# From norm 2 to the FFN: factors per token tile on VectorE, weight sums and splits made earlier, and a fixed order

## The chip, the core and the metric

The kernel runs on one core of one Trainium2 chip. A time is device microseconds (us) of one execution. The engines are TensorE (PE in the profile, its weight loads PEld), VectorE (DVE), ScalarE (ACT), GpSimd (POOL) and SyncE (SP, which here issues DMA loads).

## The reference

One layer (DEPTH = 1) over 1024 tokens of 1024 channels, float32. The part that matters here is the end of the mixer and the FFN:

```python
merged = (jax.nn.sigmoid(ga) * (y_a @ w_branch_a[l])
          + jax.nn.sigmoid(gb) * (y_b @ w_branch_b[l]))
x = x + g1 * (merged @ w_out[l])                       # output projection
h = rmsnorm(x, ln2_g[l]) * (1.0 + sc2) + sh2           # norm 2
f = (jax.nn.silu(h @ w_ffn_gate[l]) * (h @ w_ffn_up[l])) @ w_ffn_down[l]
x = x + g2 * f
```

Ahead of it stand a first norm, one input projection, stick-breaking attention (`y_a`, 16 heads) and a short gated convolution (`y_b`). The FFN's hidden width is 2816.

## The kernel before

*Split products.* Every float32 operand of a matmul is kept as two fp32r tiles: `hi`, a copy rounded by ScalarE, and `lo`, the difference, made by VectorE. A 128-deep slice of a product is three matmuls: hi x hi, hi x lo, lo x hi. `split` does this for a 512-wide piece of a weight (ScalarE L952, VectorE L953), `split_big` for activations in pieces of 1024 elements (ScalarE L963, VectorE through the helper `tt`, L128).

*The branch projection.* The second attention output is read back from DRAM in 16 tiles (`yr`, L901, two buffers, SyncE's queue), split, and multiplied by `w_a` in eight steps `m`. In one of these steps `preload_wo` loads the first pieces of the output projection's weight and splits them ahead, so that their loads stand on SyncE's queue in between.

*Output projection and norm 2.* The loop runs over two column halves `ch` and eight token tiles `i` of 128 tokens; a tile is 24 matmuls. In the second half, VectorE makes the scaled product `tm` (L1011) and the residual `x1` (L1018) of each tile. ScalarE stores the latter, squares it with a running sum (L1022) and scales it (L1024) by a root that GpSimd makes (`rstd_of`, L114 and L115). `norm2_tail` follows one tile later: eight transposes on TensorE (L971), and eight evictions into `h2b`, taken in turn by ScalarE (L979) and VectorE (L976).

*The FFN's products.* Gate and up are done by a scheme of the Strassen type. `h2b[e][n]` is the quadrant of channel half `e` and token half `n`. Seven factors `rh[q]`/`rl[q]` are made of the four quadrants; factors 0 and 1 are the first token half as it is. The others need differences: for tokens of the second half GpSimd makes two per token tile (the result `t2f` is a tile of its own), another 2048-wide one (L1089) and VectorE the last (L1092), and then `split_big` makes the factors in the order 5, 4, 2, 6, 3. `wsum` makes the four sums `s1` to `s4` of a column's weight tiles: VectorE for the first gate column, GpSimd for all others. A half product (`half_prod`, L123 to L125) is 12 matmuls, and a column of gate or up (`strassen`) is seven of them. Of three columns the two products that need only factors 0 and 1 are made ahead of the rest (`pre`), interleaved with the last token tiles' norm.

*The column loop.* `j` runs over 11 pairs of hidden tiles; ScalarE applies Silu to the gate, VectorE multiplies by up, and seven combinations (`fa`, `fb` and others) are stored to DRAM by `put_f` for the down projection.

*Order.* The framework's scheduler chooses the order on each engine from its own model of the durations; instructions with unmet needs then wait on semaphores. `in_order(i0)` instead fixes, for the instructions from number `i0` on, the order on each engine as the program has it. The kernel before calls it once, in an early stage (L310).

Of the kernel before, what the change touches and what calls it, by code (L numbers as in the profile page):

```python
# [16 lines left out]
P = 128  # L17
# [12 lines left out]
def block_kernel(tc, x, x_t, cols, ada_1, ada_2, ada_row, w_q, w_kv, w_v1, w_cg, w_a, w_b, w_o, w_g, w_u, w_d, out):  # L30
# [850 lines left out]
    def preload_wo():  # L881

        for j in range(2):
            raw = wx.tile([P, 1024], F32, tag="raw", bufs=1, name=nm("raw"))
            cn = 1024 - 512 * j
            nc.sync.dma_start(raw[:, :cn], w_o[0, j, :, :cn])
            for k in range(2 - j):
                hi = wx.tile([P, 512], F32R, tag="whi", bufs=3, name=nm("whi"))
                lo = wx.tile([P, 512], F32R, tag="wlo", bufs=3, name=nm("wlo"))
# [19 lines left out]
    for m in range(KT):  # L909
        if m == KT - 1:  # L910
            preload_wo()
# [24 lines left out]
    wp = sw.enter_context(tc.tile_pool(name="wpd", bufs=1, reuse_waits="tile"))  # L936
    s6 = ExitStack()
# [28 lines left out]
    def norm2_tail(i, xn):  # L966
        n, t0 = i // 4, (i % 4) * P
        for g in range(2):
            tr = bank()
            for j in range(4):  # L970
                nc.tensor.transpose(tr[:, j * P:(j + 1) * P], xn[:, (4 * g + j) * P:(4 * g + j + 1) * P], ident)  # L971
            for j in range(4):
                k = 4 * g + j
                o, s = h2b[g][n][:, j, t0:t0 + P], tr[:, j * P:(j + 1) * P]
# [5 lines left out]
        if n:  # L980
            b = lambda e, m: h2b[e][m][:, :, t0:t0 + P]
            nc.gpsimd.tensor_tensor(out=b(0, 1), in0=b(0, 1), in1=b(0, 0), op=ALU.subtract)
            nc.gpsimd.tensor_tensor(out=t2f[:, :, t0:t0 + P], in0=b(1, 1), in1=b(0, 1), op=ALU.subtract)

    tails = []
    for ch in range(2):
        w = [] if ch else list(w_pre)
        for j in range(len(w) // 2, 4):
            raw = load_raw(w_o[ch, j])
            w += [split(raw[:, c * 512:(c + 1) * 512]) for c in range(len(w) % 2, 2)]  # L990
        if ch == 1:
            swx.close()
            rqs.close()
            s5 = ExitStack()
            hp = s5.enter_context(tc.tile_pool(name="phh", bufs=1, side="right", reuse_waits="tile"))

            h2t = {q: hp.tile([P, 4, 512], F32, name=f"h2b{q}") for q in ("01", "11", "t2", "00", "10")}
            h2b = [[h2t[f"{e}{n}"] for n in range(2)] for e in range(2)]
            t2f = h2t["t2"]
        cs = slice(ch * 512, ch * 512 + 512)  # L1000
        for i in range(8):
            n, t0 = i // 4, (i % 4) * P
            xi = dp.tile([P, 512], F32, tag="xr", bufs=3, name=nm("xr"))
            nc.scalar.dma_start(xi, x[i * P:(i + 1) * P, cs])
            ps = bank()
            for k in range(KT):
                nc.tensor.matmul(ps, mh[n][:, k, t0:t0 + P], w[k][0], start=(k == 0), stop=False)
                nc.tensor.matmul(ps, mh[n][:, k, t0:t0 + P], w[k][1], start=False, stop=False)
                nc.tensor.matmul(ps, mlo[n][:, k, t0:t0 + P], w[k][0], start=False, stop=(k == KT - 1))
            tm = dp.tile([P, 512], F32, tag="tm", bufs=2, name=nm("tm"))  # L1010
# [12 lines left out]
            r = rstd_of(ss, 1.0 / D, dp, 1)  # L1023
            nc.scalar.activation(xn, x1, AF.Copy, scale=r[:, 0:1])  # L1024
# [10 lines left out]
    rh = [bh[:, 0:4], bh[:, 4:8], None, None, None, None, None]  # L1035
    rl = [bl[:, 0:4], bl[:, 4:8], None, None, None, None, None]
    NJ = NH // 2

# [4 lines left out]
    pre = {}  # L1043
    for key, src in (((0, 0), w_g), ((0, 1), w_u), ((1, 0), w_g)):
        raw = load_raw(src[key[0]])
        ps = bank()
        prod(ps, split(raw[:, :512]), 0)
        p2 = bank()
        prod(p2, split(raw[:, 512:]), 1)
        if tails:  # L1050
            norm2_tail(*tails.pop())
        pre[key] = (ps, p2)

    def wsum(j, e, src, eng):

        raw = load_raw(src[j])
        a11, a12 = raw[:, :512], raw[:, 512:]
        if (j, e) in pre:
            p1, p2 = pre[j, e]
        else:  # L1060
            p1, p2 = bank(), bank()
            prod(p1, split(a11), 0)
# [289 lines left out]
```

## Time and profile before

| | |
|---|---|
| median of 3 runs | 1936.05 us (1933.06 to 1937.56) |
| the profiled execution | 1933.53 us, its span 1931.8 us |
| TensorE busy | 1838.2 us, 95% |
| its weight loads | 1517.6 us, 79% |
| VectorE busy | 1452.0 us, 75% |
| ScalarE busy | 865.7 us, 45% |
| GpSimd busy | 484.4 us, 25% |
| mean granted clock of TensorE | 0.983 |
| DMA | 235 MB read, 111 MB written, 180 GB/s |

How to read the rows. A row of a timeline has the start in us from the span's start, the length of the instruction or the mean of a run of equal ones, the engine, line, operation, result and operands by name, shape, and the count; in brackets stands the wait ahead of it and what ended it. L123 to L125 are the matmuls of the FFN's half products, L1009 those of the output projection, L772 and L773 those of the branch projection; the line of VectorE's helper, L128, stands for many places, so that names and shapes tell them apart. A row of windows gives for a stretch its length, then busy time and instructions of TensorE, its weight loads, VectorE, ScalarE and GpSimd, then the mean granted clock, the share of the DMA engines, and the count of something that isn't used here.

### The profile page before, as it was taken

The numbers are of one execution on the slowest core, as the hardware profiler recorded it, in microseconds if no ns is written. First come the engines' busy times: TensorE is split into PE (matmuls) and PEld (weight loads), VectorE is DVE, ScalarE is ACT, GpSimd is POOL, SyncE is SP. The second block draws the span as 40 slices with busy tenths as digits, with TensorE's granted clock in tenths as the row PEclk, the third lists the DMA queues.
The fourth block names the chain that finished last, engine by engine and source line by source line (L and its number), as shares of the span: only waits on it lengthen the run. The fifth ranks groups of instructions, "written<-read, shape, count | busy, mean of one in ns | idle before, by whom it ended". The sixth has DMA issues, their size and how long they took to land.

```text
span 1931.8 us, 25024 instructions
## 1 busy us (share of the span) xinstructions
PE 1838.2 (95%) x8829; PEld 1517.6 (79%) x8829; DVE 1452.0 (75%) x2024; ACT 865.7 (45%) x1602; POOL 484.4 (25%) x349
## 2 busy tenths in 40 slices
PE   7799898999999899999999899979999999999999
PEld 5578776888778888887888688867888888878787
DVE  7864676878784799999999644499988788843854
ACT  4332443333333677777777321464444434422221
POOL 0484335532321000000000000055445445301013
PEclk9899998999999899999999999999999999999999
DMA  7655432224676666569653535323444334389666
GB/s 293 221 179 185 169 132 97 88 77 164 228 242 219 187 168 180 170 177 296 188 159 108 186 136 193 138 85 116 157 161 167 153 139 165 132 308 332 253 222 224
DMA packets 151148, 347.47 MB, mean 180 GB/s; under 512 B 15088, under 2 KB 52208, under 8 KB 149104
## 3 DMA queue, kind: packets, MB, share of 16 engines
q1 hardware_dynamic: 74000, 218.80, 34.4%
q10 hardware_dynamic: 76016, 123.41, 17.8%
q0 software_dynamic: 1008, 3.67, 0.5%
q8 instruction: 70, 1.15, 0.2%
q14 instruction: 54, 0.44, 0.1%
HBM read 235.19 MB, written 110.62 MB: 179 GB/s over the span
## 4 chain that ended last, share of the span: by engine, by line
PE 62%; DVE 16%; DMA 9%; issue 5%; POOL 4%; ACT 3%; ACTq 0%; SPq 0%; DVEq 0%; POOLq 0%
PE e L124 6%; PE e L123 6%; PE e L125 6%; PE pj L123 4%; PE pj L124 4%; PE pj L125 4%; PE e L1190 3%; PE e L1191 3%; DVE pt L697 3%; PE e L1189 3%; PE pj L772 3%; PE pj L773 3%; PE pj L774 3%; POOL tb L128 2%; PE pj L269 2%
## 5 line engine op out<-in xcount | busy, mean ns | idle before, releaser
L697 DVE TENSOR_TENSOR_SCAN pt<-pt,dm 128x256 f32<-128x256 f32 (+7 forms) x128 | 171.6, 1344 | 9.6 <-ACT pt L692 9.3
L114 POOL TENSOR_SCALAR rs_m<-ss 128x1 f32<-128x1 f32 x8 | 2.0, 254 | 656.4 <-ACT xn L1022 656.4
L124 PE MATMUL e<-big,whi 128*128 128x512 f32 x352 | 138.1, 392 | 7.6 <-DVE big L128 7.6
L123 PE MATMUL e<-big,whi 128*128 128x512 f32 x352 | 137.6, 391 | 1.0 <-ACT c L1105 1.0
L125 PE MATMUL e<-big,wlo 128*128 128x512 f32 x352 | 137.5, 391 | 0.0
L692 ACT ACTIVATE pt<-z,rq 128x512 f32<-128x512 f32 (+2 forms) x192 | 112.4, 586 | 44.0 <-PE z L691 19.8
L123 PE MATMUL pj<-big,whi 128*128 128x512 f32 x320 | 127.1, 397 | 1.0 <-DVE c L128 1.0
L128 POOL TENSOR_TENSOR ws<-raw,raw 128x512 f32<-128x512 f32 x41 | 58.9, 1437 | 275.6 <-DMA raw<-w_cg 135.2
L125 PE MATMUL pj<-big,wlo 128*128 128x512 f32 x320 | 126.8, 396 | 0.0
L269 PE MATMUL pj<-whi,big 128*128 128x512 f32 x352 | 111.9, 404 | 15.4 <-DVE vs L376 9.8
L1190 PE MATMUL e<-wlo,f 128*128 128x512 f32 (+1 forms) x319 | 123.0, 386 | 3.8 <-DVE wlo L953 3.8
L124 PE MATMUL pj<-big,whi 128*128 128x512 f32 x320 | 126.5, 395 | 0.0
L1191 PE MATMUL e<-whi,f 128*128 128x512 f32 (+1 forms) x319 | 122.4, 384 | 0.0
L128 DVE TENSOR_TENSOR c<-e,c 128x512 f32<-128x512 f32 x154 | 103.0, 682 | 22.6 <-PE e L125 22.5
L1189 PE MATMUL e<-whi,f 128*128 128x512 f32 (+1 forms) x319 | 116.7, 384 | 1.8 <-DMA f<-d_f 1.8
L128 DVE TENSOR_TENSOR c<-pj,c 128x512 f32<-128x512 f32 x140 | 93.5, 684 | 28.6 <-PE pj L125 28.3
L693 ACT ACTIVATE sg<-z,rq 128x512 f32<-128x512 f32 (+1 forms) x192 | 112.3, 588 | 1.1 <-PE tr L713 1.0
L419 ACT ACTIVATE whi<-raw 128x512 fp32r<-128x512 f32 x116 | 72.9, 632 | 86.3 <-PE pj L124 50.9
L128 POOL TENSOR_TENSOR ws<-raw,ws 128x512 f32<-128x512 f32 x62 | 102.5, 1653 | 22.4 <-DVE wlo L953 20.7
L128 DVE TENSOR_TENSOR wlo<-raw,whi 128x512 fp32r<-128x512 f32 x116 | 90.0, 779 | 21.3 <-ACT whi L419 19.8
L713 PE MATMUL tr<-dm,sg 128*128 128x128 f32 x576 | 92.7, 276 | 13.2 <-DVE atl L717 11.0
L124 PE MATMUL e<-rl,whi 128*128 128x512 f32 x264 | 102.8, 389 | 1.8 <-DVE rl L128 1.8
(246 smaller groups left out, 5340.1 us busy)
## 6 DMA issues: line engine op xcount, KB each, us to landing
f<-d_f SPq DMA_DIRECT2D x77, 512.0 KB, 4.4
d_f<-fs ACTq DMA_DIRECT2D x70, 512.0 KB, 2.7
raw<-w_cg SPq DMA_DIRECT2D x40, 512.0 KB, 3.5
uu<-ada ACTq DMA_DIRECT2D x32, 512.0 KB, 4.5
raw<-w_g SPq DMA_DIRECT2D x24, 512.0 KB, 3.1
raw<-w_u SPq DMA_DIRECT2D x23, 512.0 KB, 3.1
d_k<-khl ACTq DMA_DIRECT2D x32, 256.0 KB, 3.3
d_q<-gt ACTq DMA_DIRECT2D x32, 256.0 KB, 2.0
```

The lines of the kernel that those rows point to most:

```text
L123: nc.tensor.matmul(ps, wh[:, k, :], fh[:, k, :], start=(k == 0), stop=False)
L124: nc.tensor.matmul(ps, wh[:, k, :], fl[:, k, :], start=False, stop=False)
L125: nc.tensor.matmul(ps, wl[:, k, :], fh[:, k, :], start=False, stop=(k == 3))
L128: eng.tensor_tensor(out=out, in0=a, in1=b, op=op)
L269: nc.tensor.matmul(ps, a, b, start=(k == 0 and q == 0), stop=(k == KT - 1 and q == 2))
L692: nc.scalar.activation(pt[:, off + s0:off + s0 + m], z[:, :m], AF.Sigmoid, scale=rq[:, 1, i, h:h + 1])
L693: nc.scalar.activation(sg[:, s0:s0 + m], z[:, :m], AF.Sigmoid, scale=rq[:, 0, i, h:h + 1])
L697: nc.vector.tensor_tensor_scan(out=pt[:, rev], data0=pt[:, rev], data1=dm[:, rev], initial=0.0, op0=ALU.mult, op1=ALU.add)
L713: nc.tensor.transpose(tr[:, j * P:(j + 1) * P], sg[:, (b0 + j) * P:(b0 + j + 1) * P], ident)
L1189: nc.tensor.matmul(o, sh, w[0][:, c], start=(j == 0), stop=False)
L1190: nc.tensor.matmul(o, sh, w[1][:, c], start=False, stop=False)
L1191: nc.tensor.matmul(o, sl, w[0][:, c], start=False, stop=(j == NJ - 1))
```

## The change

1. *Branch projection.* `preload_wo` runs one step `m` earlier, and loads three pieces with five splits, instead of two with three.
2. *Weight sums.* The four sums of the first gate column are made by VectorE in the first half of the output projection, into tiles `wt` of a new pool that last to the end of the FFN. The second load of that column's weight comes later for its plain products, so 1 MB of weights is read twice.
3. *Factors.* `tail_f` makes them for each token tile of the second half: five VectorE operations of 128x4x128 and one ScalarE copy. Factor 2 is split there at once, into a pool of its own; the differences are left in `h2b`. GpSimd's differences and `t2f` go.
4. *The last two token tiles.* Tile 6's transposes come inside tile 7's 24 matmuls (at `k == 5`), and its evictions and `tail_f(6)` ahead of VectorE's first operation for tile 7. The split of the second half of the first gate weight stands behind the square of tile 7.
5. *Behind the projection.* The two plain products of three columns, `two(...)`, are made as before; the splits of the four ready sums (`sps`) come in between, and the first gate column's remaining products run in the order 6, 5, 3, 7, 4, each behind its factor.
6. *Fixed order.* `in_order(i0)` covers all this, from the last token tile's start to the split of factor 3.
7. *The column loop.* `c11` of a gate is added up at once and put into `wt` tile 0; `fa` and `fb` go into `wt` tiles 2 and 3.

```diff
-        for j in range(2):
+        for j in range(3):
             raw = wx.tile([P, 1024], F32, tag="raw", bufs=1, name=nm("raw"))
...
-                hi = wx.tile([P, 512], F32R, tag="whi", bufs=3, name=nm("whi"))
+                hi = wx.tile([P, 512], F32R, tag="whi", bufs=5, name=nm("whi"))
...
-        if m == KT - 1:
+        if m == KT - 2:
             preload_wo()
...
+    def tail_f(i, qs=(0, 1)):
+        t0 = (i % 4) * P
+        b = lambda e, m: h2b[e][m][:, :, t0:t0 + P]
+        if 0 in qs:
+            h_, l_ = (r[:, :, t0:t0 + P] for r in (rh[2], rl[2]))
+            tt(nc.vector, b(0, 1), b(0, 1), b(0, 0), ALU.subtract)
+            nc.scalar.activation(h_, b(1, 1), AF.Copy)
+            tt(nc.vector, l_, b(1, 1), h_.bitcast(F32), ALU.subtract)
+            tt(nc.vector, b(1, 1), b(1, 1), b(0, 1), ALU.subtract)
+        if 1 in qs:
+            tt(nc.vector, b(0, 0), b(1, 1), b(0, 0), ALU.subtract)
+            tt(nc.vector, b(1, 0), b(1, 0), b(1, 1), ALU.subtract)
...
-        if n:
-            b = lambda e, m: h2b[e][m][:, :, t0:t0 + P]
-            nc.gpsimd.tensor_tensor(out=b(0, 1), in0=b(0, 1), in1=b(0, 0), op=ALU.subtract)
-            nc.gpsimd.tensor_tensor(out=t2f[:, :, t0:t0 + P], in0=b(1, 1), in1=b(0, 1), op=ALU.subtract)
+        if i > 3:
+            late_f.append(i)
+            while i > 4 and late_f:
+                tail_f(late_f.pop(0))
...
+        if ch == 0:
+            ws0 = [wt(q) for q in range(4)]
+            w_sums(load_raw(w_g[0]), load_raw(w_g[NJ]), *ws0, nc.vector)
...
+            last = (ch, i) == (1, 7)
+            if last:
+                i0 = len(nc.cur_bb.bb.instructions)
+                raw00 = load_raw(w_g[0])
+                s00 = split(raw00[:, :512])
...
             for k in range(KT):
+                if last and k == 5:
+                    trs = tail_tr(tails.pop()[1])
...
+            if last:
+                tail_ev(6, trs)
+                tail_f(6)
             tm = dp.tile([P, 512], F32, tag="tm", bufs=2, name=nm("tm"))
...
             r = rstd_of(ss, 1.0 / D, dp, 1)
+            if last:
+                s00b = split(raw00[:, 512:])
...
+    pq[1], pq[2] = two(s00, s00b)
+    s01 = halves(load_raw(w_u[0]))
+    trs = tail_tr(tails.pop()[1])
...
-    split_big(rh[5], rl[5], t2f)
-    split_big(rh[4], rl[4], h2b[0][1])
-    nc.gpsimd.tensor_tensor(out=h2b[0][0], in0=t2f, in1=h2b[0][0], op=ALU.subtract)
-    split_big(rh[2], rl[2], h2b[1][1])
+    sps = [split(ws0[q]) for q in (1, 0, 3, 2)]
+    pre[0, 1] = two(*s01)
+    x1p, x11 = wt(1), wt(0)
+    nc.scalar.activation(x1p, pq[1], AF.Copy)
+    tt(nc.vector, x11, pq[2], x1p, ALU.add)
+    s10 = halves(load_raw(w_g[1]))
+    tail_ev(7, trs)
+    tail_f(7, (0,))
+    pre[1, 0] = two(*s10)
+    split_big(rh[5], rl[5], h2b[1][1])
+    pq[6] = product(sps[0], 5)
+    split_big(rh[4], rl[4], h2b[0][1])
+    pq[5] = product(sps[1], 4)
+    tail_f(7, (1,))
+    pq[3] = product(sps[2], 2)
     split_big(rh[6], rl[6], h2b[0][0])
-    nc.vector.tensor_tensor(out=h2b[1][0], in0=h2b[1][0], in1=t2f, op=ALU.subtract)
+    pq[7] = product(sps[3], 6)
+    sp4 = split(load_raw(w_g[NJ])[:, 512:])
     split_big(rh[3], rl[3], h2b[1][0])
+    in_order(i0)
...
-        nc.scalar.activation(c11, p1, AF.Copy)
...
-        tt(nc.vector, c11, p2, c11, ALU.add)
+        c11 = ct("c01", 1) if e else wt(0)
...
+        nc.scalar.activation(c21, p1, AF.Copy)
+        tt(nc.vector, c11, p2, c21, ALU.add)
```

The new lines `tail_tr` and `tail_ev` are the two parts of the old `norm2_tail`, and `product` and `two` wrap `half_prod` with a PSUM bank each. Three places show how the instructions move. In these rows a name is followed by its numbers, `e` is a PSUM bank, `raw` a loaded weight, `whi` and `wlo` its split, `rh` and `rl` a factor, `big` a pair of factors.

VectorE at the last token tile, before (`tm_2439` and `x1_2440` are tile 7's):

```order
L1011 TENSOR_TENSOR tm_2439_11962<-e_2438_11937,g1b_11198 128x512
L953 TENSOR_TENSOR wlo_2469_12109<-raw_2463_12088,whi_2468_12108 128x512
L1018 TENSOR_TENSOR x1_2440_11964<-tm_2439_11962,xr_2437_11935 128x512
L976 TENSOR_SCALAR h2b01_11521<-e_2445_11976,a2_11200,mod_104 128x128
L976 TENSOR_SCALAR h2b11_11522<-e_2446_11985,a2_11200,mod_104 128x128
L128 TENSOR_TENSOR raw_2470_12124<-raw_2470_12124,raw_2471_12126 128x512
L128 TENSOR_TENSOR s2_12128<-raw_2471_12126,raw_2470_12124 128x512
L128 TENSOR_TENSOR raw_2471_12126<-raw_2471_12126 128x512
L128 TENSOR_TENSOR raw_2470_12124<-raw_2470_12124,s2_12128 128x512
L976 TENSOR_SCALAR h2b01_11521<-e_2445_11976,a2_11200,mod_104 128x128
L976 TENSOR_SCALAR h2b11_11522<-e_2446_11985,a2_11200,mod_104 128x128
```

VectorE there, after (`tm_2450` and `x1_2451` are tile 7's):

```order
L982 TENSOR_SCALAR h2b01_11541<-e_2448_11986,a2_11213,mod_104 128x128
L128 TENSOR_TENSOR h2b00_11543<-h2b11_11542,h2b00_11543 128x4x128
L128 TENSOR_TENSOR h2b10_11544<-h2b10_11544,h2b11_11542 128x4x128
L982 TENSOR_SCALAR h2b11_11542<-e_2449_11987,a2_11213,mod_104 128x128 x2
L128 TENSOR_TENSOR h2b01_11541<-h2b01_11541,h2b00_11543 128x4x128
L128 TENSOR_TENSOR rl2_11537<-h2b11_11542,rh2_11536 128x4x128
L128 TENSOR_TENSOR h2b11_11542<-h2b11_11542,h2b01_11541 128x4x128
L128 TENSOR_TENSOR h2b00_11543<-h2b11_11542,h2b00_11543 128x4x128
L128 TENSOR_TENSOR h2b10_11544<-h2b10_11544,h2b11_11542 128x4x128
L1064 TENSOR_TENSOR tm_2450_12019<-e_2447_11970,g1b_11211 128x512
L1071 TENSOR_TENSOR x1_2451_12021<-tm_2450_12019,xr_2446_11968 128x512
L955 TENSOR_TENSOR wlo_2457_12033<-raw_2443_11962,whi_2456_12032 128x512
```

Tile 7's two operations stood ahead of tile 6's four evictions (L976) and the four weight sums; now they stand behind tile 6's evictions (L982) and the factor operations of tiles 5 and 6 (128x4x128).

ScalarE from the last residual's store on, before:

```order
L1019 DMA d_x1_80<-x1_2440_11964 128x512
L1022 ACTIVATE xn_2442_11969,ss_2441_11968<-x1_2440_11964 128x1024
L979 ACTIVATE h2b01_11521<-e_2445_11976,mod_104,a2_11200 128x128
L979 ACTIVATE h2b11_11522<-e_2446_11985,mod_104,a2_11200 128x128
L952 ACTIVATE whi_2479_12254<-s2_12128 128x512
L1024 ACTIVATE xn_2442_11969<-x1_2440_11964,rs_r_2444_11972 128x1024
L952 ACTIVATE whi_2482_12273<-raw_2471_12126 128x512
L952 ACTIVATE whi_2485_12291<-raw_2470_12124 128x512
L952 ACTIVATE whi_2488_12310<-raw_2470_12124 128x512
L952 ACTIVATE whi_2491_12328<-raw_2471_12126 128x512
```

And after:

```order
L1072 DMA d_x1_80<-x1_2451_12021 128x512
L1075 ACTIVATE xn_2453_12026,ss_2452_12025<-x1_2451_12021 128x1024
L954 ACTIVATE whi_2456_12032<-raw_2443_11962 128x512
L1079 ACTIVATE xn_2453_12026<-x1_2451_12021,rs_r_2455_12029 128x1024
L954 ACTIVATE whi_2461_12065<-raw_2460_12063 128x512
L954 ACTIVATE whi_2463_12069<-raw_2460_12063 128x512
L954 ACTIVATE whi_2469_12093<-wt_2324_11232 128x512
L954 ACTIVATE whi_2471_12097<-wt_2323_11231 128x512
L954 ACTIVATE whi_2473_12101<-wt_2326_11234 128x512
L954 ACTIVATE whi_2475_12105<-wt_2325_11233 128x512
L1125 ACTIVATE wt_2479_12135<-e_2458_12037 128x512
L1203 ACT_TABLE_LOAD
```

The evictions of tile 6 (L979) stood behind the square; now only a weight split (L954) stands between the square and the scaling of tile 7, and six more splits, a copy and the table load follow ahead of tile 7's evictions.

SyncE in the branch projection, before:

```order
L886 DMA raw_2296_11103<-w_o 128x512
L901 DMA yr_2192_10512<-d_ya0_72 128x512
L901 DMA yr_2194_10517<-d_ya1_73 128x512
L735 DMA d_ya1_73<-oy_2170_10395 64x256
L901 DMA yr_2196_10522<-d_ya1_73 128x512
L901 DMA yr_2198_10527<-d_ya1_73 128x512
L735 DMA d_ya1_73<-oy_2173_10423 64x256
L915 DMA sgi_2215_10567<-d_sga_74 128x512
L901 DMA yr_2200_10532<-d_ya1_73 128x512
```

And after:

```order
L886 DMA raw_2285_11027<-w_o 128x1024
L901 DMA yr_2192_10512<-d_ya0_72 128x512
L901 DMA yr_2194_10517<-d_ya1_73 128x512
L735 DMA d_ya1_73<-oy_2170_10395 64x256
L886 DMA raw_2290_11037<-w_o 128x512
L901 DMA yr_2196_10522<-d_ya1_73 128x512
L735 DMA d_ya1_73<-oy_2173_10423 64x256
L901 DMA yr_2198_10527<-d_ya1_73 128x512
L915 DMA sgi_2215_10567<-d_sga_74 128x512
```

The output weight's pieces (`w_o`) are now three, and the third stands ahead of the third `yr` load behind the second piece.

More of the change, by code (lines that the diff above doesn't have):

```diff
@@ L936, in block_kernel @@
     wp = sw.enter_context(tc.tile_pool(name="wpd", bufs=1, reuse_waits="tile"))
+    stp = ExitStack()
+    tp = stp.enter_context(tc.tile_pool(name="pht", bufs=1, reuse_waits="tile"))
     s6 = ExitStack()
@@ L1096, in block_kernel, with wsum @@
     cp = s7.enter_context(tc.tile_pool(name="phc2", bufs=1, side="right", reuse_waits="tile"))
+    def wsum(j, e, src, eng):
+        raw = load_raw(src[j])
+        p1, p2 = pre[j, e] if (j, e) in pre else two(*halves(raw))
+        raw2 = load_raw(src[j + NJ])
+        ws = [cp.tile([P, 512], F32, tag=f"ws{q}", bufs=1, name=nm("ws")) for q in range(4)]
+        w_sums(raw, raw2, *ws, eng)
+        return (p1, p2, *ws, raw2[:, 512:])
     def ct(tag, bufs):
```

106 lines of the change are left out of this document (57 added, 49 removed).

## The prediction

> **What bounds the kernel now.** I read the page's slices first (TensorE at nine tenths or more except near slice 28), then the 4 us windows of that dip, and then each engine's timeline through it. TensorE from the last tokens of the output projection to the second FFN column:
>
> ```profile
> 1271.40 0.39 PE L1009 MATMUL e<-whi,big 128*128 128x512 f32 x1
> 1272.70 1.09 PE L971 MATMUL e<-dm,xn 128*128 128x128 f32 x8 [0.91 <-ACT xn L1024]
> ...
> 1281.10 1.09 PE L971 MATMUL e<-dm,xn 128*128 128x128 f32 x8 [1.82 <-ACT xn L1024]
> ...
> 1300.58 0.79 PE L124 MATMUL e<-big,whi 128*128 128x512 f32 x1 [7.04 <-DVE big L128]
> 1301.18 0.63 PE L125 MATMUL e<-big,wlo 128*128 128x512 f32 x1
> ...
> 1310.68 0.50 PE L124 MATMUL e<-rl,whi 128*128 128x512 f32 x1 [1.75 <-DVE rl L128]
> ...
> 1318.75 0.39 PE L123 MATMUL e<-big,whi 128*128 128x512 f32 x1
> ...
> 1332.35 0.39 PE L123 MATMUL e<-big,whi 128*128 128x512 f32 x1
> ```
>
> The last two rows are 60 matmuls apart: 0.227 us each. From 1271.6 (end of the projection's issue) to 1318.75 TensorE does 132 matmuls (6 half products ahead, 5 products) and two groups of transposes at 0.85 us: 31.6 us of work in 47.1. So 15.5 us is all that this stage can give back, 0.8% of the time; it is waits for VectorE, and a clock that falls behind the long one:
>
> ```profile
> 1296.00:1300.00 4.00, 0.00 (x0) 0.00 (x0) 4.00 (x2) 1.65 (x2) 4.00 (x3) 0.69 0.00 0
> 1300.00:1304.00 4.00, 3.42 (x8) 2.74 (x9) 4.00 (x3) 2.85 (x4) 3.92 (x3) 0.50 0.00 0
> ```
>
> In both windows VectorE (third busy figure) is at 4.00 of 4.00 and GpSimd (fifth) nearly so; the granted clock is 0.50 in the second. What fills VectorE:
>
> ```profile
> 1256.76 2.36 DVE L128 TENSOR_TENSOR big<-h2b,big 128x1024 fp32r<-128x1024 f32 x2 [0.54 <-ACT big L963]
> ...
> 1265.38 0.69 DVE L1011 TENSOR_TENSOR tm<-e,g1b 128x512 f32<-128x512 f32 x1 [1.11 <-PE e L1009]
> ...
> 1275.88 0.68 DVE L1018 TENSOR_TENSOR x<-tm,xr 128x512 f32<-128x512 f32 x1
> ...
> 1278.77 0.69 DVE L128 TENSOR_TENSOR raw<-raw 128x512 f32<-128x512 f32 x1
> ...
> 1291.69 6.63 DVE L1092 TENSOR_TENSOR h2b<-h2b,h2bt 128x2048 f32<-128x2048 f32 x1
> 1298.24 4.51 DVE L128 TENSOR_TENSOR big<-h2b,big 128x1024 fp32r<-128x1024 f32 x2
> ...
> 1307.14 4.62 DVE L128 TENSOR_TENSOR rl<-h2b,rh 128x1024 fp32r<-128x1024 f32 x4
> ```
>
> ```profile
> 1290.76 5.41 POOL L1089 TENSOR_TENSOR h2b<-h2bt,h2b 128x2048 f32<-128x2048 f32 x1
> 1296.12 3.32 POOL L128 TENSOR_TENSOR ws<-raw,raw 128x512 f32<-128x512 f32 x1
> ```
>
> A 1024-wide split takes 1.15 us with GpSimd idle (1256.76, 1307.14) and 2.25 beside it (1298.24). A 512-wide operation alone starts its follower 0.60 later.
>
> The profiled execution took 1933.53 us (span 1931.8); the runs' median is 1936.05, 2.5 above it. I add the change to both.
>
> **The change, step by step.** What leaves GpSimd (eight 512-wide differences and a 2048-wide one, 12 units of 512) becomes 12 x 0.60 = 7.2 us of VectorE. The weight sums (four times 0.60) move ahead of the stage, to where VectorE waits for TensorE; they cost nothing there while that slack lasts, else 2.4 us. In return VectorE runs beside an idle GpSimd: 6.63 for 2048 elements instead of some 2.4, and 2.2 more for the pair at 1298. The engine's load thus falls a little; what counts is the order, and I walk it with the rows above and these of ScalarE:
>
> ```profile
> 1241.24 1.06 ACT L1022 ACTIVATE xn<-x 128x1024 f32<-128x1024 f32 x1 [0.49 <-DVE h2b L976]
> ...
> 1242.30 0.79 ACT L979 ACTIVATE h2b<-e,mod,a 128x128 f32<-128x128 f32 x2
> 1243.34 1.15 ACT L1024 ACTIVATE xn<-x,rs_r 128x1024 f32<-128x1024 f32 x1 [0.24 <-POOL rs_r L115]
> ...
> 1280.95 2.18 ACT L952 ACTIVATE whi<-raw 128x512 fp32r<-128x512 f32 x4
> ...
> 1298.35 3.90 ACT L963 ACTIVATE rh<-h2b 128x1024 fp32r<-128x1024 f32 x4 [5.62 <-DVE h2b L1092]
> ...
> 1307.93 1.28 ACT L1136 ACT_TABLE_LOAD   x1
> ```
>
> *Token tile 6.* VectorE takes it at 1265.4 as before, but with one factor operation of tile 4 in between: residual done at 1267.2. Then 0.4 for a store's issue, the square 1.2, GpSimd's root 0.9 and the scaling 1.15 (the rows of 1241.24 to 1243.34, 3.3 us from the square's start to the scaling's end): 1271.1. TensorE reaches the transposes, now after 15 of tile 7's 24 matmuls, at 1266.1 + 3.4 = 1269.5: a wait of 1.6.
>
> *Token tile 7.* Its first VectorE operation now stands behind tile 6's evictions (four of 0.4, each pair waiting for ScalarE's, about 0.5 more), three factor operations of tile 5 and five of tile 6 (eight of 0.6): from 1272.3 to 1279.4. The residual is done at 1280.7, against 1276.5 in the row of 1275.88: 4 us later. Behind it in ScalarE's queue: store, square (1282.4), split of the second half of the first gate weight (1283.0), scaling (1284.5). TensorE ends the projection at 1274.0 and the first half product at 1276.8, and now waits for that split: 6.2 us, where the old order had the product ready. By the row of 1301.18 the clock is then halved for some 8 matmuls, 0.2 us each: 1.7 us.
>
> *The factors.* ScalarE next has six weight halves (0.52 each), a copy, the table load and a Silu, then two halves more: 1291.1. Four alternating evictions: 1294.6. Tile 7's three factor operations and a copy: 1296.8. Then, at 0.95 on ScalarE and 1.15 on VectorE, the splits of factors 5 and 4 (to 1302.6), two differences, factor 6 (1306.8), a weight half, factor 3. TensorE by then does transposes, 48 matmuls of the two `pre` pairs and the products, with no wait of note: it ends the fourth at 1310.4 or before, the fifth at 1313.0.
>
> *The next column.* GpSimd's sums for the first `up` column lie in the memory of a factor that is read until 1306.8: four operations, done near 1313, beside factor 3's two splits (2.0 instead of 1.15 each, to 1311.7). VectorE then has nine sums (0.60) and only behind them the low halves that TensorE's next products need: 1317.9. TensorE starts six matmuls at 1316 (a wait of 3.0) and goes on at 1317.9.
>
> So TensorE stands at 1317.9 where it stood at 1318.75 + 6 x 0.227 = 1320.1: a gain of 2.2 us. The first slow stretch costs nothing, since the fifth product's end is followed by a wait anyway. A second one behind the 3.0 us wait has no cover: 0 or 1.7, and I take 1.0, since 2.28 us was enough once:
>
> ```profile
> 1099.17 0.94 PE L772 MATMUL pj<-ya,whi 128*128 128x512 f32 x2 [2.28 <-ACT ya L905]
> 1099.91 0.63 PE L773 MATMUL pj<-ya,whi 128*128 128x512 f32 x1
> ```
>
> but the waits of 1.82 and 1.75 above were not. [...]
>
> *The branch projection.* `preload_wo` loads three pieces, one position earlier, and the third stands on SyncE's queue ahead of the second half of the attention output:
>
> ```profile
> 1075.39 0.33 SPq L886 DMA_DIRECT2D raw<-w_o  x1
> ...
> 1080.58 0.95 SPq L901 DMA_DIRECT2D yr<-d_ya  x2
> ...
> 1098.49 0.63 ACT L905 ACTIVATE ya<-yr 128x512 fp32r<-128x512 f32 x1 [4.64 <-DMA yr<-d_ya]
> 1100.96 0.63 ACT L905 ACTIVATE ya<-yr 128x512 fp32r<-128x512 f32 x1 [0.80 <-DMA yr<-d_ya]
> ```
>
> It waits for two splits, so the pair issued at 1080.58 leaves some 0.7 later, and the chain of loads up to 2 us. Against that TensorE's order there changes: the matmuls that waited 2.28 us come behind nine of the next column, so that at the old arrival times about 1.2 us of waits would remain, in pieces, and no slow stretch (8 x 0.2). Ends: a gain of 2.7, a loss of 2. I take a gain of 1.3, nearer the first, for the arrivals are bounded by loads already two deep.
>
> The extra reads (1 MB of weights loaded twice) and the other preloads lie beside full TensorE work: nothing, or at most a landing of some 3 us if a buffer comes free late. In the FFN's later columns TensorE had only the wait of 0.99 at 1349.83, which I leave standing:
>
> ```profile
> 1349.83 0.50 PE L123 MATMUL e<-big,whi 128*128 128x512 f32 x1 [0.99 <-ACT c L1105]
> ```
>
> Sum: 2.2 - 1.0 + 1.3 = 2.5 us less: 1931.0 for a profiled execution, 1933.5 for the median. Bounds: all waits gone, 15.5 + 2.7; all against it, about 5 us more.
>
> **The rivals.**
> *The waits do go* (0.22). If the last token's residual comes by 1277, TensorE finds the split at 1279 and the factors 4 us earlier: 6 to 12 us less, 1924 to 1930. Against it speaks the order of VectorE shown above; for it, that eight of the operations in front are priced from other shapes.
>
> *It gets slower* (0.12). GpSimd's sums start when their weights land, near 1295, and not behind factor 6. Then six splits are at 2.25 instead of 1.15, 6.6 us, and the end of that stage saves 2.0: the gain of 2.2 turns into a loss of 2.4, with 1.7 for the clock 4.1: 1938 to 1941. It decides from the moment that more than two splits run beside GpSimd. Row 1298.24 gives the price; the memory of the sums speaks against the place. [...]
>
> *Nothing is left of it* (0.14). The slow stretch comes in full and the branch projection gives nothing: 2.2 - 1.7 = 0.5, 1935 to 1937. The waits have then only changed their place.
>
> **How the numbers follow.** 0.2% is 3.9 us, about what a measurement of this kernel can tell from no change. The forecast has 0.52, of which 0.18 lies below 1932.2. Faster: 0.18 + 0.22 = 0.40. Slower: 0.10 of the slow rival. Same: the remaining 0.50. The range reaches from the middle of the first rival, 1925, to the slow one's lower part, 1939.
>
> **What the new profile would show.** Right: a TensorE wait of about 6 us near 1277 to 1283 released by ScalarE's split, followed by a clock of 0.5; a wait of 1 to 2 us before the transposes inside tile 7; one of about 3 us near 1314; VectorE's 1024-wide splits at 1.15 up to factor 6; GpSimd's first sum after it. Wrong: the residual of tile 7 by 1277, or GpSimd busy from 1295, or a wait over 3 us at the branch projection.

## The result and the profile after

The changed kernel is slower: 1953.93 us median (1948.5 to 1961.13, 4 runs) against 1934.55 (1924.7 to 1937.56), a ratio of 1.0108 with a 95% interval of 1.0084 to 1.0132. The profiled execution has a span of 1950.0 us against 1931.8.

Executions differ by several us before the output projection begins: its first matmul starts at 1177.09 and 1182.88 us in two profiles of code that is the same up to it. So I count from that matmul on: 754.7 us before (1931.8 - 1177.09), 774.8 after (1950.0 - 1175.17), 20.1 more. The main waits of TensorE from there to the down projection's start, in its timeline:

```profile
1270.19 1.09 PE L972 MATMUL e<-dm,xn 128*128 128x128 f32 x8 [1.87 <-ACT xn L1079]
...
1282.09 0.79 PE L123 MATMUL e<-big,whi 128*128 128x512 f32 x1 [5.98 <-ACT whi L954]
...
1315.49 0.50 PE L123 MATMUL e<-big,whi 128*128 128x512 f32 x1 [2.50 <-DVE c L128]
...
1348.57 0.72 PE L123 MATMUL e<-big,whi 128*128 128x512 f32 x1 [2.19 <-ACT c L1172]
...
1714.90 0.77 PE L1258 MATMUL e<-whi,f 128*128 128x512 f32 x1 [3.35 <-DMA f<-d_f]
...
1729.74 0.77 PE L1258 MATMUL e<-whi,f 128*128 128x512 f32 x1 [9.38 <-DMA f<-d_f]
```

The first three are those that the prediction named. The fourth, in column 1, was 0.99 before. The last two lie 360 us behind the stage that was changed: TensorE waits for loads of `f`, the FFN's result, from DRAM. Before the change the same two matmuls waited 1.03 and 0.77 us:

```profile
1710.19 0.47 PE L1189 MATMUL e<-whi,f 128*128 128x512 f32 x1 [1.03 <-DMA f<-d_f]
...
1713.94 0.47 PE L1189 MATMUL e<-whi,f 128*128 128x512 f32 x1 [0.77 <-DMA f<-d_f]
```

Behind each of the long waits the clock is low as well: 0.50 at 1716 to 1720 us, behind the first, and 0.70 at 1732 to 1736, behind the second. The first of these windows (the clock is the third figure from the end):

```profile
1716.00:1720.00 4.00, 4.00 (x11) 2.87 (x9) 3.10 (x5) 1.34 (x3) 1.60 (x3) 0.50 0.37 143
```

SyncE's queue says what held the loads (columns: who waited for whom, total us, times, longest), first after the change, then before it:

```profile
SPq L1242 <- PE e L125: 40.6, 2, 38.9
SPq L1233 <- PE e L1260: 15.9, 6, 5.3
SPq L1233 <- DVE fs L128: 12.6, 1, 12.6
```

```profile
SPq L1173 <- PE e L125: 39.9, 2, 37.9
SPq L1164 <- PE e L1191: 19.9, 10, 3.1
SPq L1164 <- PE e L125: 6.8, 2, 4.3
```

The first row of each, loads of the down projection's weights, is not new. New is that one load of `f` (L1233) waited 12.6 us for VectorE's last operation of `put_f`. In the built program two buffers of `f`, the second load's among them, now lie at the addresses of the last column's `c` tiles, and the first one on factor 3, which is read to the very end of the FFN; before, the first ones lay on factors 2 and 3. And within the FFN, the 36 matmuls with factors 6, 2 and 3 of one column (first matmul of each dozen, and the first of the next product):

```profile
1396.78 0.39 PE L123 MATMUL e<-rh,whi 128*128 128x512 f32 x1
...
1399.50 0.40 PE L123 MATMUL e<-rh,whi 128*128 128x512 f32 x1
...
1402.30 0.39 PE L123 MATMUL e<-rh,whi 128*128 128x512 f32 x1
...
1405.04 0.39 PE L123 MATMUL e<-big,whi 128*128 128x512 f32 x1
```

Before the change, the products with factors 2 and 3:

```profile
1379.88 0.39 PE L123 MATMUL e<-rh,whi 128*128 128x512 f32 x1
...
1382.60 0.39 PE L123 MATMUL e<-rh,whi 128*128 128x512 f32 x1
...
1385.32 0.39 PE L123 MATMUL e<-big,whi 128*128 128x512 f32 x1
```

The product with factor 2 takes 2.80 us, that with factor 6 takes 2.72, as every product before; the one with factor 3 takes 2.74, and only its first matmuls are late. The tiles of factor 2 are now at 212960 and 221152 bytes, 480 modulo 512; before they were at multiples of 512. The 20.1 us, in order of place:

| stretch | before | after | difference |
|---|---|---|---|
| output projection to the end of column 0's `up` | 155.3 | 154.6 | -0.6 |
| column 1 (gate and `up`) | 33.9 | 37.0 | +3.0 |
| the other 18 half columns, to the FFN's end | 342.9 | 344.8 | +1.9 |
| from there to the end of the span | 222.6 | 238.4 | +15.8 |

### The profile page after: what moved, and what is told of

Its sections match the earlier page's. It is cut to its first block, busy times and chain, and to the rows that moved or that the text cites. A ratio compares the mean times of both kernels' runs of the same rounds, so it can differ in the third digit from the quotient of the medians.

```text
span 1950.0 us, 25049 instructions
## 1 busy us (share of the span) xinstructions
PE 1847.2 (95%) x8829; PEld 1521.9 (78%) x8829; DVE 1437.6 (74%) x2041; ACT 867.2 (44%) x1604; POOL 466.5 (24%) x340
## 3 DMA queue, kind: packets, MB, share of 16 engines
q8 instruction: 70, 1.15, 0.2%
## 4 chain that ended last, share of the span: by engine, by line
PE 65%; DVE 15%; DMA 6%; issue 5%; POOL 4%; ACT 4%; ACTq 0%; SPq 0%; DVEq 0%; POOLq 0%
PE e L123 6%; PE e L124 6%; PE e L125 6%; PE pj L123 5%; PE pj L125 5%; PE pj L124 5%; PE e L1259 3%; PE e L1260 3%; PE e L1258 3%; PE pj L772 3%; PE pj L773 3%; PE pj L774 3%; DVE pt L697 3%; POOL tb L128 2%; PE pj L269 2%
## 5 line engine op out<-in xcount | busy, mean ns | idle before, releaser
L128 DVE TENSOR_TENSOR c<-e,c 128x512 f32<-128x512 f32 x142 | 94.9, 683 | 53.7 <-PE e L125 53.7
L1258 PE MATMUL e<-whi,f 128*128 128x512 f32 (+1 forms) x319 | 118.2, 389 | 12.7 <-DMA f<-d_f 12.7
L717 DVE TENSOR_TENSOR atl<-tr,ath 128x512 fp32r<-128x512 f32 (+1 forms) x192 | 100.4, 542 | 6.8 <-ACT ath L716 6.4
L713 PE MATMUL tr<-dm,sg 128*128 128x128 f32 x576 | 93.2, 277 | 12.3 <-DVE atl L717 10.9
L123 PE MATMUL e<-rh,whi 128*128 128x512 f32 x264 | 103.6, 392 | 0.0
```

Source lines behind the costliest of these rows:

```text
L123: nc.tensor.matmul(ps, wh[:, k, :], fh[:, k, :], start=(k == 0), stop=False)
L128: eng.tensor_tensor(out=out, in0=a, in1=b, op=op)
L717: nc.vector.tensor_tensor(out=tl[:, :nb, c0:c0 + P], in0=src, in1=th[:, :nb, c0:c0 + P].bitcast(F32), op=ALU.subtract)
L1258: nc.tensor.matmul(o, sh, w[0][:, c], start=(j == 0), stop=False)
```

## The experiments

The framework stacks its tile pools from both ends of the on-chip memory; the left side begins at the low addresses, and the change puts factor 2's pool on the right. "Left" means the changed kernel with factor 2 on the left side. Each ratio is to runs of the kernel before that were taken with the experiment (medians of 1932.88 us for 1 to 4, 1931.01 for 5 to 8, 1932.11 for 9 to 12; the changed kernel's is to 1934.55). The last two columns come from one profile each. The last column counts from the projection's first matmul to the end of the span, the one ahead of it to the end of column 1.

| kernel | median us | ratio to before | to column 1 | to the end |
|---|---|---|---|---|
| before | | | 189.2 | 754.7 |
| changed | 1953.93 | 1.0108 [1.0084, 1.0132] | 191.6 | 774.8 |
| 1 left | 1935.69 | 1.0015 [0.9999, 1.0030] | 191.5 | 756.9 |
| 2 padded by 32 | 1953.84 | 1.0103 [1.0076, 1.0130] | 190.2 | 773.3 |
| 3 `f` placed otherwise | 1937.99 | 1.0030 [1.0008, 1.0053] | 190.0 | 756.7 |
| 4 before, factors off by 32 | 1940.15 | 1.0037 [1.0019, 1.0055] | 189.8 | 762.0 |
| 5 before, off by 64, 128, 256 | 1939.31 (one run) | | 189.7 | 759.8 |
| 6 left, `c21` in turn | 1935.68 | 1.0027 [1.0012, 1.0041] | 191.0 | 755.9 |
| 7 left, tile 7 first | 1936.23 | 1.0013 [0.9996, 1.0031] | 191.5 | 756.4 |
| 8 left, order free | 1925.66 | 0.9956 [0.9935, 0.9977] | 178.7 | 743.1 |
| 9 as 8, preloaded weights at multiples of 512 | 1922.30 | 0.9952 [0.9934, 0.9970] | 178.0 | 742.9 |
| 10 changed, order free | 1941.72 | 1.0047 [1.0029, 1.0065] | 178.3 | 762.4 |
| 11 as 8, differences on GpSimd | 1924.90 | 0.9960 [0.9943, 0.9977] | 179.5 | 744.7 |
| 12 as 8, sums in the stage | 1924.71 | 0.9959 [0.9944, 0.9974] | 179.9 | 745.9 |

**1. Factor 2 on the left.**

```diff
+    sr2 = ExitStack()                      # ahead of the projection's pool, and closed behind it
+    r2p = sr2.enter_context(tc.tile_pool(name="phr2", bufs=1, reuse_waits="tile"))
-            r2p = sr2.enter_context(tc.tile_pool(name="phr2", bufs=1, side="right", reuse_waits="tile"))
```

> The changed kernel with one edit: the pool of factor 2 (rh2, rl2) lies on the left side of the memory instead of the right, with the same instructions in the same order on every engine. It moves factor 2 from an address of 32 modulo 64 bytes to one of 0, and gives the last column's c tiles back the place behind the first buffers of f. Theory (both losses are places in memory): the first two f loads of the down projection no longer wait for the last column, TensorE's waits there fall from 3.35 and 9.38 to about 1.0 and 0.8 and the slow clock behind them goes, some 13 to 16 us; and the products with factor 2 go from 0.236 to 0.227 us per matmul, 2.3 us over 22 products: 1950.0 becomes 1931 to 1934 for the profiled span, so no slower than before. Rival (the later start of the down projection is VectorE's and the DMA queues' own, from the second reading of the weights and the later end of the column): the waits of 3.35 and 9.38 stay, and at most 2.3 us is gained, 1947 to 1950.

17.9 us come back. SyncE no longer waits for `put_f`. The first two matmuls that waited for `f` now wait 0.62 us, for a weight split of ScalarE, and 0.16 us, for the load. The waits of SyncE's queue and the first matmul of the down projection:

```profile
SPq L1242 <- PE e L125: 40.3, 2, 38.5
SPq L1233 <- PE e L1260: 21.4, 11, 2.7
SPq L1233 <- PE e L125: 6.1, 2, 5.0
```

```profile
1711.93 0.47 PE L1258 MATMUL e<-whi,f 128*128 128x512 f32 x1 [0.62 <-ACT whi L956]
```

A half column takes 19.04 us again instead of 19.15. Same instructions, same order: the loss behind column 1 is a matter of places alone, and since this run moves both places, experiments 3 and 4 take them apart. But the kernel is then level with the old one, not faster; column 1 still ends 2.3 us later than before.

**2. The right side shifted by 32 bytes.**

```diff
+            pad = r2p.tile([P, 8], F32, name="pad")
```

> The changed kernel with 32 bytes of padding in the pool of factor 2, so that all tiles of the right side lie at 0 modulo 64 bytes instead of 32, with the same instructions in the same order; the f buffers still overlap the last column's tiles. Theory (an operand at 32 modulo 64 is read more slowly): the 12 matmuls of each product with factor 2 take 0.227 us each instead of 0.236, as the others do, 0.107 us less per column and 2.0 to 2.4 us less in all: span about 1947.7. The waits of 3.35 and 9.38 at the down projection stay. Rival (the side or the upper part of the memory is slower, or traffic of other engines to that tile): the spacing stays at 0.236 and the span at 1950.

The rival held as far as the number goes: the second dozen still takes 2.80 us (1399.45 to 1402.25). It does not show that the side is at fault, since the tiles were then at 448 modulo 512; in experiment 9, with tiles on the right side at multiples of 512, 24 matmuls take 5.44 us, 0.227 each.

```profile
1396.73 0.39 PE L123 MATMUL e<-rh,whi 128*128 128x512 f32 x1
...
1399.45 0.39 PE L123 MATMUL e<-rh,whi 128*128 128x512 f32 x1
...
1402.25 0.39 PE L123 MATMUL e<-rh,whi 128*128 128x512 f32 x1
```

**3. The buffers of `f` elsewhere.** Two `wdx` tiles, then the six `f`, then the other `wdx`:

```diff
+    wdx = [e2.tile([P, 1024], F32, name=nm("wdx")) for n in range(2)]
+    f_first = [f_tile()]
+    wdx += [e2.tile([P, 1024], F32, name=nm("wdx")) for n in range(2 * NJ - 18)]
```

> The changed kernel with only the places of the down projection's tiles exchanged: two of the spare weight tiles wdx come first, then the six buffers of f, then the other four wdx, so that no f buffer lies over the last column's c tiles; same instructions in the same order. Theory: the second f load issues some 10 us earlier, the waits of 3.35 and 9.38 fall to 1 to 2 us together, and 12 to 16 us are gained: span 1934 to 1938. The products with factor 2 stay at 0.236. Rival (the stores of the last column, or the queues, hold the loads back): the f loads issue where they did and the span stays within 2 us of 1950.

As the theory had it: waits of 0.47 and 0.53 instead of 3.35 and 9.38, 18.1 us less from the projection on, and 2.80 us for factor 2 as in the changed kernel. Of the 18.1, 1.6 came up to column 1, where TensorE's clock did not fall this time: behind the wait of 2.17 us its matmuls start 0.23 us apart.

```profile
1714.71 0.47 PE L1262 MATMUL e<-whi,f 128*128 128x512 f32 x1 [0.47 <-DMA f<-d_f]
...
1718.24 0.47 PE L1262 MATMUL e<-whi,f 128*128 128x512 f32 x1 [0.53 <-DMA f<-d_f]
```

**4. The old kernel with its factors off by 32 bytes.**

```diff
+    pad = ep.tile([P, 8], F32, name="pad")
     for q in (6, 2, 3):
```

> The kernel before the change with 32 bytes of padding ahead of the six tiles of factors 6, 2 and 3, which then all lie at 32 modulo 64 bytes; nothing else differs, same instructions in the same order. Theory: three of the seven products of each column go from 0.2267 to about 0.2355 us per matmul, 36 x 0.0088 = 0.32 us per column and 7 us over 22 columns: span 1931.8 becomes about 1939. Rival (the address alone costs nothing): spacing 0.2267 and no change.

All three products of each column go to 2.80 us, and the ratio is 1.0037 with its interval above 1: on the left side too an address off the multiples of 512 bytes costs. The span grows by 7.3 us from the projection on, 7 expected, but the agreement is in part luck: the 18 half columns behind column 1 give 5.0 of it (0.28 each, 0.32 expected) and the part behind the FFN, which does not read the factors, another 1.7.

```profile
1383.63 0.40 PE L123 MATMUL e<-rh,whi 128*128 128x512 f32 x1
...
1386.43 0.39 PE L123 MATMUL e<-rh,whi 128*128 128x512 f32 x1
...
1389.23 0.39 PE L123 MATMUL e<-rh,whi 128*128 128x512 f32 x1
...
1392.03 0.40 PE L123 MATMUL e<-big,whi 128*128 128x512 f32 x1
```

**5. Which grid?** Three offsets in one kernel:

```diff
+    for q, pad in ((6, 16), (2, 16), (3, 32)):
+        ep.tile([P, pad], F32, name=f"pad{q}")
```

> The kernel before the change with padding inside the pool of its factor tiles: factor 6 lies at 64 modulo 128 bytes, factor 2 at 128 modulo 256, factor 3 at 256 modulo 512; same instructions in the same order. The run with 32 bytes ahead of all three gave 0.2336 us per matmul against 0.2264, the one that moved factor 2 of the changed kernel from 32 to 64 (modulo 128) gave no change. Theory: the operand wants an address of a multiple of 128 bytes or more: factor 6 stays slow at 0.2336, factors 2 and 3 go to 0.2264 (or 2 also stays slow, if 256 is wanted). Rival (64 is enough, and the changed kernel's factor 2 is slow from the right side or upper part of the memory): all three at 0.2264.

A half column takes 19.21 us against 19.04 aligned and 19.32 with all at 32. The three products take 2.76 (64 modulo 128), 2.80 (128 modulo 256) and about 2.77 us (256 modulo 512). So neither reading was right: factor 2 at 128 is as slow as at 32, and mine stopped at 128 or 256. For 256 it is not settled, since a product behind a slow one takes 2.74 to 2.76 even at a multiple of 512 (the one with factor 3 in the changed kernel, the first of the next column in experiment 4), little less than 2.77. In all runs here only tiles at multiples of 512 bytes gave 2.72.

**6. A second place for `c21`.**

```diff
+        c21 = wt(1) if j % 2 and not e else ct(f"c1{e}", 1)
```

> The changed kernel with factor 2 on the left (as in the first run), and of its gate columns every odd one writes c21 into the free weight tile 1 instead of a tile of its own, so that the copy of the first product need not wait for GpSimd's reading of the column before. Theory (the gain up to column 1 is given back there, since the copy on ScalarE waits for GpSimd's combinations and the PSUM banks of the two plain products are held meanwhile): the wait of 2.38 us in column 1 (0.99 before the change, 2.19 to 2.4 after) goes or falls below 0.5, and with the slow clock behind it 2 to 4 us are gained over the first run: span 1930 to 1932. Rival (GpSimd's weight sums for that column are late themselves): another wait of about 2 us takes its place within the column and the span stays at 1933 to 1934.

The rival: TensorE no longer waits for ScalarE's copy, but in the same column for a split of `put_f` on ScalarE. Column 1 ends 0.5 us earlier than in experiment 1.

```profile
1354.48 0.47 PE L123 MATMUL e<-big,whi 128*128 128x512 f32 x1 [1.99 <-ACT fs L1197]
```

**7. Tile 7 ahead of tile 6's factors**, and the first weight's two halves split together:

```diff
             if last:
                 tail_ev(6, trs)
-                tail_f(6)
...
+            if last:
+                tail_f(6)      # behind tile 7's scaling
```

> The changed kernel with factor 2 on the left, and tile 7's residual ahead of tile 6's factor operations on VectorE (five of 0.6 us), and the second half of the first weight split together with the first, ahead of tile 7. Theory of the prediction (tile 7's chain stands behind tile 6's factors, and the wait of 6 us for a weight split behind its square is a matter of the order): the residual comes 3 us earlier, the wait of 4.4 to 6.0 falls below 2, and of this 2 to 4 us are left at the end of column 0 and at the end of the run: span 1930 to 1932. Rival (VectorE and GpSimd bound what follows): the wait of 2.4 to 2.8 behind the fourth product grows by what the first loses and the span stays at 1933 to 1934.

The rival again. The wait of 4.4 to 6 us went and came back in pieces (one more, of 2.44, stands ahead of tile 6's transposes), and column 1 ends at the same 191.5.

```profile
1283.84 1.10 PE L974 MATMUL e<-dm,xn 128*128 128x128 f32 x8 [0.41 <-ACT xn L1079]
1287.75 0.50 PE L125 MATMUL e<-big,wlo 128*128 128x512 f32 x1 [2.13 <-DVE wlo L957]
1299.59 0.50 PE L124 MATMUL e<-big,whi 128*128 128x512 f32 x1 [0.76 <-DVE big L128]
1316.99 0.50 PE L123 MATMUL e<-big,whi 128*128 128x512 f32 x1 [3.40 <-DVE c L128]
```

**8. Without the fixed order.**

```diff
-    in_order(i0)
```

> The changed kernel with factor 2 on the left and without the fixed order from the last token tile on: the scheduler places these instructions. It shows what the fixed order is worth by itself. Theory (the order is worth little, since the same work of VectorE bounds the stage): end of the first column within 2 us of the first run, span 1932 to 1937. Rival (the order carries the gain): the stage ends 4 us later or more, span above 1938.

Both readings fell, in the direction that I had not written down: 12.8 us less up to column 1, and the kernel is now faster than before the change (0.9956, the interval below 1). Of the 12.8, 9.2 lie ahead of column 1. In column 1 itself the wait is 0.40 where the changed kernel has 2.19 and experiment 1 has 2.38:

```profile
1343.40 0.50 PE L123 MATMUL e<-big,whi 128*128 128x512 f32 x1 [0.40 <-ACT c L1171]
```

**10. Without the fixed order, the places as in the change.** The same edit on the changed kernel:

> The changed kernel as it is, with factor 2 on the right and the f buffers over the last column's tiles, but without the fixed order. Theory (order and places add up): the end of column 1 comes 10 to 13 us earlier than in the changed kernel, as in the version on the left, while the products with factor 2 stay at 2.80 us per 12 matmuls and the waits of the down projection at 10 us or more: span 1937 to 1942, so still slower than before. Rival (the down projection's waits hang on when the loads start, so that an earlier stage lets them vanish): 1926 to 1930.

Order and places add up: 13.3 us less up to column 1 than the changed kernel, and the waits for `f` are still there (3.36 and 9.83 us). The orders can be read in the 40 us that begin 80 us after the projection's first matmul. Before the change, the changed kernel, then without the fixed order (length, busy time and count of TensorE, weight loads, VectorE, ScalarE, GpSimd; clock):

```profile
1257.09:1297.09 40.00, 33.37 (x160) 26.65 (x158) 36.17 (x43) 27.53 (x45) 21.18 (x16) 1.00 0.29 99
```

```profile
1255.17:1295.17 40.00, 31.78 (x143) 25.27 (x143) 31.29 (x54) 26.65 (x46) 2.88 (x6) 0.91 0.25 87
```

```profile
1256.67:1296.67 40.00, 36.74 (x176) 29.65 (x175) 38.34 (x63) 34.90 (x56) 4.60 (x6) 1.00 0.25 86
```

And what VectorE waited for in the last two, the longest rows:

```profile
DVE wlo L955 <- ACT whi L954: 4.8, 3, 2.1
DVE h2b L982 <- ACT h2b L985: 1.8, 4, 0.5
DVE rl L128 <- ACT rh L994: 1.2, 1, 1.2
```

```profile
DVE rl L128 <- ACT rh L994: 0.7, 1, 0.7
DVE big L128 <- ACT big L965: 0.5, 1, 0.5
```

In the fixed order VectorE stands still for 8.7 of the 40 us, 4.8 of it for weight halves that ScalarE has not made yet; the longest of these waits, 2.1 us, is for the half that stands behind tile 7's square in ScalarE's queue. Without it these splits come earlier, around tile 7's two operations. VectorE then stands still for 1.7 us, and 176 matmuls are done; in the fixed order it is 143, fewer than the 160 of the old kernel. It also ran the product with factor 2, which is ready first, ahead of all but the first matmuls of those with 5 and 4. That the order costs the 13 us is shown, twice, by one line taken out. That it does so through these gaps is read from the two profiles and not tested: which of the single exchanges is worth how much was not tried, except for experiment 7, which was worth nothing by itself.

**9. The preloaded weights at multiples of 512 too.** `preload_wo` puts its five splits at 480 modulo 512:

```diff
+        wx.tile([P, 120], F32, name="wxpad")
```

> The version without the fixed order and with factor 2 on the left, with 480 bytes of padding behind the preloaded pieces of the output projection's weight, so that these five splits lie at multiples of 512 bytes instead of 480 modulo 512; same instructions in the same order. Theory (a moving operand off a multiple of 512 bytes is read more slowly): of 24 matmuls of each token tile of the first half, 15 use these pieces; they go from 0.232 to 0.227 us, a tile from 5.54 to 5.47, 0.5 to 0.6 us in all. Rival: tiles stay at 5.54. Against the kernel before: faster by 6 to 10 us.

A token tile of the first half goes from 5.54 to 5.44 us, of which 0.8 us are left up to column 1 and 0.2 at the end. This version has the lowest median, 1922.3 us, 0.9952 of before (0.9934 to 0.9970) and 9.8 us below it, though the ratios do not tell this version from 8, 11 and 12. What is shown is the tile's time.

**11. The differences back on GpSimd.**

```diff
-            tt(nc.vector, b(0, 1), b(0, 1), b(0, 0), ALU.subtract)
+            tt(nc.gpsimd, b(0, 1), b(0, 1), b(0, 0), ALU.subtract)   # and the three others
```

> The version without the fixed order and with factor 2 on the left, but the four differences of each token tile on GpSimd instead of VectorE (16 operations of 512; the split of factor 2 stays on VectorE). Theory (with the order free the gain comes from VectorE's load being spread, not from which engine makes the differences): VectorE loses 16 x 0.60 = 9.6 us of work, GpSimd gets 16 x 1.3 to 2.2 = 21 to 35 us beside VectorE's splits, the last token tile's factors come 2 to 5 us later and the span is 1926 to 1930. Rival (the differences on VectorE were the whole of the gain): the stage is as long as before the change, 1932 or more.

The end comes 1.6 us later than in experiment 8, by the times not to be told from it (0.9960 against 0.9956). GpSimd makes all four differences here, where the old kernel gave it part of them. With the order free, which engine makes the differences, a main point of the change, matters little.

**12. The sums in the stage.**

```diff
+    w_sums(load_raw(w_g[0]), load_raw(w_g[NJ]), *ws0, nc.vector)
     sps = [split(ws0[q]) for q in (1, 0, 3, 2)]
```

> The version without the fixed order and with factor 2 on the left, but the four sums of the first gate column are made where their splits stand, in the stage itself, and not in the first half of the output projection. Theory (the prediction's step: ahead they cost nothing, in the stage four times 0.60): VectorE has 2.4 us more in the stage, which has hardly any idle time left, so column 1 ends 2 to 3 us later: span 1926 to 1928. Rival (TensorE has slack there): no change, 1924.

Column 1 ends 1.2 us later than in experiment 8, the end 2.8; the medians do not tell it apart. The expected reason is not what the profile shows: up to the end of column 0 it is 0.8 us ahead of experiment 8, and what it loses it loses in column 1, where TensorE waits 2.42 us instead of 0.40 for the same copy. So the gain of the free versions is neither the sums' alone nor that of taking the differences from GpSimd. What else carries it (factors per token tile, the order of the products) was not taken apart.

## Why the prediction was wrong

The step that failed is the last of its change part: "The extra reads (1 MB of weights loaded twice) and the other preloads lie beside full TensorE work: nothing, or at most a landing of some 3 us if a buffer comes free late", with "the wait of 0.99 at 1349.83, which I leave standing". By it the sum takes everything behind the first column as unchanged. There 20.7 us were lost (3.0, 1.9 and 15.8), most of them on just such a buffer that comes free late, at five times the 3 us and in a stage that the prediction does not look at.

- *The new pools' places* (+15.8 and +1.9, no term in the sum). Part 3 of the change puts factor 2 into a pool that outlives the column loop, and part 7 puts tiles into a pool under it. I priced their operations and not the addresses. Experiments 1 and 3 give the 15.8 back; 1 gives the 1.9 back, and 4 shows that the address alone costs. Of the 15.8, 10.9 are the two waits (12.7 us against 1.8); the matmuls between them take 5.5 us at the low clock instead of 3.0. No rival reached down to the down projection, so the range could not hold the time.
- *Column 1* (+3.0, taken as 0). The wait grew from 0.99 to 2.19 and the clock fell behind it (0.74 at 1350 to 1354 us). In experiment 3 the wait is 2.17 and the clock stays; there the column loses 1.4, so about half of the 3.0 is the clock. Why the wait grew is open. That TensorE comes to it earlier is not enough: in 8 it comes nine us earlier still and waits 0.40. Moving one of the waits (6) brought 0.5 us up to there.
- *The stage itself* had its waits sized well: 1.87, 5.98 and 2.50 us stand where 1.6, 6.2 and 3.0 were forecast; the residual of tile 7 ends 6.7 us behind the projection's end, as forecast; the splits up to factor 6 take 1.15 to 1.18 us each, and GpSimd's first sum starts at 1305.64, right behind factor 6. So all the signs of being right came, and the reason of the rival "it gets slower" did not: the signs looked at this stage alone. The terms of the sum were less good. Where it has TensorE 2.2 us ahead, TensorE is 0.9 ahead, and 0.6 at the end of column 0. The second slow stretch (taken at 1.0) did not come behind the wait of 2.50 (a clock of 1.00 at 1315 to 1319 us); the first lasted 12 matmuls, 0.43 us apart, not 8; and the projection's first half takes 50.0 us instead of 49.5, since five preloaded pieces and not three lie off the multiples of 512 bytes (49.1 in experiment 9).
- *The branch projection* (forecast a gain of 1.3): none shown, and a small loss. From its first matmul with `w_a` to the output projection's first it takes 91.4, 87.4 and 87.2 us in the three profiles of the old code (before, 4 and 5), and only the first of them has the wait of 2.28 on which the forecast rested; it takes 88.7 to 91.1 us in the eleven profiles of the new code. Its second half takes 44.5 us in all eleven, against 43.5 in the three, with a wait that the old code does not have:

```profile
1175.17 0.50 PE L1057 MATMUL e<-whi,big 128*128 128x512 f32 x1 [0.78 <-DVE sgi L920]
```

This 1 us lies ahead of the matmul from which I count, and is not in the 20.1.

- *The order.* The prediction says that the order is what counts, walks the one written out, and does not ask what another order of the same work would give. With the order free (8), the first rival ("the waits do go") came to pass with its own condition: the residual of tile 7 ends 99.8 us behind the projection's first matmul, which is 1276.9 in the old profile's count (by 1277, it said), and 11.6 us are gained from the projection on, where it had 6 to 12.

## What to carry to other kernels

When a change adds a pool or lengthens the life of one, list what its tiles' addresses push aside, to the end of the kernel: which later buffer now lies on a tile that is read late, and whether every matmul operand still starts where it ran at full rate. When a change writes an order out by hand, run it once without: here the hand order cost 13 us, more than the 11.6 that the change brought without it. And compare two profiles from a landmark just ahead of the change, not from the start.

## What the runs showed of the hardware

The 512-wide operand of a matmul (128x512 fp32r; the other is the 128x128 of the weight load) off a multiple of 512 bytes made a dozen matmuls take 2.76 to 2.80 us instead of 2.72. It was so for the FFN's factors on both sides of the memory (2.80 on each), and the projection's preloaded weights on the right made a tile of 24, 15 of them with such an operand, take 5.54 against 5.44 us. Factors at 32, 128, 448 and 480 modulo 512 took 2.80, at 64 2.76; 256, with 2.77, is not settled, and narrower operands and the 128x128 ones were not tried.

Whether the clock falls behind a wait of 2 to 3 us does not follow from the wait's length here: it fell behind waits of 2.19 us (changed kernel, 0.74 granted), 2.28 (before, 0.57 at 1099 to 1103 us), 2.44 (experiment 7, transposes of 1.97 us instead of 1.09) and 2.51 (8, 0.73 at 1284 to 1288), and not behind others of 2.17 (3) and 2.81 (2), with matmuls mostly 0.23 us apart, and of 2.50 (changed kernel and 10, 1.00). The same transposes after the same wait ran at a clock of 1.00 once and of 0.73 once (without the fixed order, changed places first, then left):

```profile
1281.41 1.09 PE L972 MATMUL e<-dm,xn 128*128 128x128 f32 x8 [2.50 <-ACT xn L1079]
```

```profile
1285.87 1.97 PE L974 MATMUL e<-dm,xn 128*128 128x128 f32 x8 [2.51 <-ACT xn L1079]
```
